# Eighteen stores of a hybrid encoder layer: issued by SyncE in place of ScalarE

## The chip, the cores and the metric

The kernel runs on one core of a Trainium2 chip. The metric is the device time of one execution in microseconds. A core has five engines with a queue of instructions each, worked off in order: TensorE (PE in the profile, its weight loads PEld), VectorE (DVE), ScalarE (ACT), GpSimd (POOL) and SyncE (SP). SyncE computes nothing; it issues transfers (DMA). ScalarE can issue transfers as well, from the same queue as its computing instructions. In the profile a queue's own work has a q behind the name: ACTq, SPq.

## The reference

One layer over 1040 tokens (16 meta tokens and 1024 of the sequence) of width 1024. A normalised input is projected once, and three mixers read the parts of the projection: a pooling mixer (256 columns), forgetting attention (6 heads of 64) and stick-breaking attention (6 heads of 64). Their outputs are concatenated, projected, added to the residual, and a SwiGLU network and a last norm follow.

```python
    for i in range(DEPTH):
        a = rmsnorm(h, norm1[i])
        proj = a @ w_in[i]
        u, qf, kf, vf, fl, qs, ks_, vs = jnp.split(proj, IN_SPLITS, axis=-1)
        y_pool = multiscale_pool_mixer(u, pool_w[i], pool_scale[i])
        ...
        y_fox = head_rmsnorm(y_fox, fox_out_gain[i], FOX_HEADS)
        ...
        y_sb = head_rmsnorm(y_sb, sb_out_gain[i], SB_HEADS)
        h = h + jnp.concatenate([y_pool, y_fox, y_sb], axis=-1) @ w_out[i]
        a = rmsnorm(h, norm2[i])
        h = h + (jax.nn.silu(a @ w_gate[i]) * (a @ w_up[i])) @ w_down[i]

    h = rmsnorm(h, final_norm)
    return h[:, N_META:N_META + s_len]
```

All inputs and the output are float32. The kernel keeps that accuracy by splitting each operand of a product into a rounded part and a rest (names with h and l: `wh`, `wl`, `ph`, `pl`, `dh`, `dl`) and adding three products.

## The kernel before, in words

The span has four parts: the input and its first projections, up to about 90 us; the mixers, to about 600 us; the SwiGLU network's first half, to about 1045 us; and its second half with the last norm. The change lies in the second part.

There the twelve heads are worked as six pairs, `p` = 0 to 5, in the order stick-breaking, three of forgetting attention, two of stick-breaking. For each pair `attention` computes scores (`sb_scores`, `fox_scores`), transposes them on TensorE, casts and subtracts them into two parts (lines 547 and 548, `ph` and `pl`), and multiplies by the values (line 533). When the two heads of a pair have half of the sequence (512 tokens) ready, `head_norm` normalises it: a square, two matmuls, logarithm and exponential on ScalarE, and a last multiply on VectorE (line 435) into the tile `yo`. `yo` has the tag `nt`, a ring of two tiles that the intermediate results of `head_out` (line 401) and of the norm use too. For the first five pairs `yo` is stored to a scratch tensor in HBM, `ysd` (line 572): ten stores of 256 KB. The sixth pair stays on the core.

Beside the attention runs a second stream, `filler`: the projections of the next pair (line 292), the two column blocks of the pooling mixer (`pool_pieces`) and the first parts of the output projection. The pooling mixer makes its output in four pieces for each of two blocks; ScalarE scales a piece out of PSUM (line 627) into a tile of tag `e`, a ring of three shared with the stick-breaking scores, and it is stored to `ysd` (line 628): eight stores of 124 to 132 KB. The output projection loads the halves of `ysd` again (`split_y`, line 697).

SyncE issues the loads of this part: the weights of the projections in pieces of 128 KB into a ring of four (`wr`, line 163; GpSimd splits each piece and so frees its buffer, line 167), the pool weights (line 614), the output weights and the scratch tensors' halves.

The order of instructions on each engine is not the order of the source. The framework's scheduler takes the whole program (`schedule_with_timeline_sim=True`), plays it through a model of the chip and gives each engine its next instruction by priority among those whose inputs and buffers are ready in the model. The function `interleave` sets how the two streams mix, and attention has a priority boost of 300. Semaphores are placed by the framework.

Of the kernel before, what the change touches and what calls it, by code (L numbers as in the profile page):

```python
# [30 lines left out]
def hymba_trunk(  # L31
# [19 lines left out]
    nc = tc.nc  # L51
# [12 lines left out]
    def T(p, shape, dt, tag, bufs=1):  # L64
        uid[0] += 1
        return p.tile(list(shape), dt, tag=tag, bufs=bufs, name=f"{tag}_{uid[0]}")
# [9 lines left out]
    def hi_pool(o, i):  # L76
        G.tensor_scalar(o, i, 1.0, 0.0, ALU.mult, ALU.add)
# [13 lines left out]
    def mm(tag, shape, bufs):  # L91
        return T(ps, shape, F32, tag, bufs)
# [82 lines left out]
    def wload(c):  # L175
        return wflat([wpart(c, hf) for hf in range(4)])
# [219 lines left out]
    def head_out(po, h, op):  # L396

        n = op.shape[1]
        a, b = 64 * h, 64 * (1 - h)
        t = T(at, [128, 512], F32, "nt", 2)  # L400
        S.copy(t[a:a + 64, :n], po[b:b + 64, :])
        V.tensor_tensor(op[a:a + 64, :], po[a:a + 64, :], t[a:a + 64, :n], ALU.add)
# [96 lines left out]
    def fox_bias(hd):  # L499
        cb = T(r1, [128, L], F32, "cb", 1)  # L500
        for t0, n in KPIECES:
            p = mm("s", [128, 512], SB_)
            PE.matmul(p[:, :n], sel[:, hd:hd + 1].to_broadcast([128, 128]), csum[:, t0:t0 + n], start=True, stop=True)
            S.copy(cb[:, t0:t0 + n], p[:, :n])
        return cb
# [22 lines left out]
    def weighted(pr, h, t, ptiles, po):  # L528
        nkb = 2 * t + 3

        def av(kb, xs, c, first):
            for ix, x in enumerate(xs):
                PE.matmul(po[:, c:256], pr.v[h][:, kb, :], x, start=first and ix == 0,  # L533
                          stop=(kb == nkb - 1 and ix == 1), skip_group_check=True)

        for g in range(0, nkb, 2):
            group = [(kb, ii) for kb in range(g, min(g + 2, nkb)) for ii in range(kb == nkb - 1, 2)]
            n = 128 * len(group)  # L540
            tp = mm("s", [128, 512], SB_)
            for i, (kb, ii) in enumerate(group):
                k0 = NM + 128 * (kb - 1) if kb else 0
                PE.transpose(tp[:, 128 * i:128 * i + 128], ptiles[ii][:, k0:k0 + 128], ident)  # L544
            ph = T(ap_, [128, 512], F32R, "ph", 3)
            pl = T(ap_, [128, 512], F32R, "pl", 3)
            S.copy(ph[:, :n], tp[:, :n])  # L547
            V.tensor_tensor(pl[:, :n], tp[:, :n], ph[:, :n], ALU.subtract)  # L548
            for kb in range(g, min(g + 2, nkb)):
                c = 128 if kb == nkb - 1 else 0  # L550
                a = 256 * (kb - g)
                av(kb, (ph[:, a:a + 256 - c], pl[:, a:a + 256 - c]), c, kb == 0)
            if kb < nkb - 1:
                yield 0.5

    def attention():

        pend = []
        cb = None
        ops = None  # L560

        def back(p, h, t, pts):
            fox, _, hd, c = PAIRS[p]
            po = mm("o", [128, 256], OB)
            yield from weighted(prs[p], h, t, pts, po)
            j, tt = t // 2, t % 2
            head_out(po, h, ops[j][:, 256 * tt:256 * tt + 256])
            if h == 1 and tt == 0:
                yo = T(at, [128, 512], F32, "nt", 2)
                head_norm(ops[j], c - 2, yo, p == 5 and j == 0, prs[p].lt[j] if fox else None)  # L570
                if p < 5:
                    nc.scalar.dma_start(ysd[c][:, 512 * j:512 * j + 512], yo)
                else:

                    yh, yl = [T(at, [128, 512], F32R, "q1", 6) if j else T(x0, [128, T0], F32R, "xb", 8)[:, :512]
                              for _ in range(2)]
                    (hi_pool if j else S.copy)(yh, yo)
                    V.tensor_tensor(yl, yo, yh, ALU.subtract)
                    last_y[j] = (yh, yl)
                    if j == 1:  # L580
                        yield None
            yield 0.5

        for p in range(6):
            fox, _, hd, c = PAIRS[p]
            if p:
                yield None
            if p == 5:
                seq = [(h, t) for t in (3, 2, 1, 0) for h in range(2)]
            else:  # L590
                seq = [(h, t) for h in range(2) for t in (3, 2, 1, 0)]
            for i, (h, t) in enumerate(seq):
                if fox and t == 3:
                    cb = fox_bias(hd + h)
                yield from (fox_scores if fox else sb_scores)(prs[p], h, t, cb)
                cur = (p, h, t, prs[p].pt)
                if i == 0:
                    while pend:
                        yield from back(*pend.pop(0))
                    ops = [T(at, [128, 512], F32, "op", 2) for _ in range(2)]  # L600
                pend.append(cur)
                while len(pend) > (DEEP[i] if p == 5 else 1):
                    yield from back(*pend.pop(0))
        while pend:
            yield from back(*pend.pop(0))


    def pool_pieces(ci):

        w = wload(ci)  # L610
        pw = T(ap_, [128, 512], F32, "e", 3)[:, :128]
        V.memset(pw, 0.0)
        for g in range(2):
            nc.sync.dma_start(pw[64 * g:64 * g + 64, 64 * g:64 * g + 64], pool_w[2 * ci + g])
        pwh = T(ap_, [128, 128], F32R, "pwh")
        S.copy(pwh, pw)
        pwl = T(ap_, [128, 128], F32R, "pwl")
        V.tensor_tensor(pwl, pw, pwh, ALU.subtract)
        late = []

        def mix(s0, n, dh, dl):
            p = mm("mm", [128, 512], MMB)
            PE.matmul(p[:, :n], pwh, dh[:, :n], start=True, stop=False)
            PE.matmul(p[:, :n], pwh, dl[:, :n], start=False, stop=False)
            PE.matmul(p[:, :n], pwl, dh[:, :n], start=False, stop=True)
            yo = T(ap_, [128, 512], F32, "e", 3)
            S.activation(yo[:, :n], p[:, :n], AF.Copy, scale=psc[:, ci:ci + 1])
            nc.scalar.dma_start(ysd[ci][:, s0:s0 + n], yo[:, :n])

        last = T(ap_, [128, NM], F32, "last")  # L630
        for t0, m in ((0, 264), (248, 280), (512, 272), (768, 272)):
            c0 = NM if t0 else 0
            o = []
            yield from proj_piece(w, t0 + c0, m - c0, o)
            u = T(at, [128, 512], F32, "pt", 3)
            if t0:
                G.tensor_copy(u[:, :NM], last)
            V.tensor_tensor(u[:, c0:m], o[0][:, :m - c0], rbc[:, t0 + c0:t0 + m], ALU.mult)
            if t0 + m < L:
                last = T(ap_, [128, NM], F32, "last")  # L640
                G.tensor_copy(last, u[:, m - NM:m])

            lv = []
            cur = u
            for lev in range(4 if ci else 2):
                sft = 1 << lev
                st = 2 * sft - 1
                nx = T(ap_, [128, 512], F32, "e", 3)
                lo = 64 if lev == (3 if ci else 1) else 0
                V.tensor_tensor(nx[lo:128, st:m], cur[lo:128, st:m], cur[lo:128, st - sft:m - sft], ALU.add)  # L650
                cur = nx
                lv.append(nx)
            n = m - NM
            dd = T(ap_, [128, 512], F32, "r", 3)
            for g in range(2):
                win = 2 << (2 * ci + g)
                r = slice(64 * g, 64 * g + 64)
                V.scalar_tensor_tensor(dd[r, :n], lv[-2 + g][r, NM:m], 1.0 / win, u[r, NM:m],
                                       ALU.mult, ALU.subtract)
            dh = T(ap_, [128, 512], F32R, "r", 3)  # L660
            hi_pool(dh[:, :n], dd[:, :n])
            dl = T(ap_, [128, 512], F32R, "r", 3)
            V.tensor_tensor(dl[:, :n], dd[:, :n], dh[:, :n], ALU.subtract)
            while late:
                mix(*late.pop())
            late.append((t0, n, dh, dl))
            yield 0.5
        while late:
            mix(*late.pop())
        yield 0.5  # L670
# [98 lines left out]
    ysd = {c: dpool.tile([128, SEQ], F32, name=f"ysd{c}") for c in range(8)}  # L769
# [446 lines left out]
```

## Time and profile before

| | |
|---|---|
| median of 3 runs | 1276.68 us (1276.63 to 1276.91) |
| profiled execution, its own time | 1277.83 us |
| its span, first to last instruction | 1275.8 us |
| mean granted clock of TensorE | 0.986 |
| TensorE busy | 1214.6 us |
| ScalarE busy | 624.4 us |
| issues of the 18 stores, on ScalarE's queue | 0.326 us each (median) |

Busy times count an engine's computing instructions; the issuing of a transfer is not among them. The chain of work that ended last is followed back from the last instruction, at each step to what released it; an engine with a small share in it can be slow at no cost. A timeline's row gives the start, the length, the engine, the line of the kernel, the operation, the tiles written and read, and in brackets the idle time before it with what ended it.

### The profile page before, as it was taken

To read this page: it belongs to the slowest core of one execution; us is meant where nothing else is said; L and a number is where in the kernel's file an instruction comes from. 1 tells how busy PE (TensorE), PEld (TensorE's weight loads), DVE (VectorE), ACT (ScalarE), POOL (GpSimd) and SP (SyncE) were. 2 spreads that over 40 slices of the span, in tenths; PEclk is the share of its full clock that TensorE was granted. 3 is DMA by queue.
4 is the path that set the end of the run, shared out by engine and by line. 5 is a ranking of instruction groups with operands and counts; after the bars stand their busy time and mean duration, and the time that the engine had idled before them with its cause. 6 is when DMAs were issued, how large, how long until landed. Compare 5 with 4: busy or idle time off the path is not lost.

```text
span 1275.8 us, 18424 instructions
## 1 busy us (share of the span) xinstructions
PE 1214.6 (95%) x6358; PEld 1024.7 (80%) x6358; DVE 915.9 (72%) x1568; ACT 624.4 (49%) x1272; POOL 489.5 (38%) x554
## 2 busy tenths in 40 slices
PE   6799899999899989999999999999999999999996
PEld 5588788889888877788787888888888888788885
DVE  8668975657947679998787677666767656866557
ACT  6366754545537677777744233233233324444443
POOL 6459245462355774550105444434444401000002
PEclk9899999999998999999999999999999999999999
DMA  5100011010101161201514554444555448576653
GB/s 181 41 9 30 19 48 34 30 38 18 47 30 34 34 219 64 78 26 50 205 42 158 190 168 169 141 130 152 190 173 165 140 140 323 174 229 196 190 169 140
DMA packets 73145, 147.12 MB, mean 115 GB/s; under 512 B 9052, under 2 KB 21340, under 8 KB 73052
## 3 DMA queue, kind: packets, MB, share of 16 engines
q1 hardware_dynamic: 69728, 142.01, 33.8%
q10 hardware_dynamic: 3324, 3.95, 0.9%
q8 instruction: 50, 0.82, 0.3%
q14 instruction: 43, 0.35, 0.1%
HBM read 103.98 MB, written 41.94 MB: 114 GB/s over the span
## 4 chain that ended last, share of the span: by engine, by line
PE 76%; DVE 14%; ACT 4%; issue 4%; DMA 1%; POOL 0%; POOLq 0%; SPq 0%; DVEq 0%; ACTq 0%
PE s L901 22%; PE mm L292 13%; PE s L1081 10%; PE mm L901 8%; PE mm L712 4%; PE o L533 4%; DVE r L490 3%; PE s L544 3%; PE mm L1081 3%; PE o L1081 3%; PE s L449 1%; DVE P L492 1%; DVE pl L548 1%; PE s L451 1%; DVE x L714 1%
## 5 line engine op out<-in xcount | busy, mean ns | idle before, releaser
L901 PE MATMUL s<-t,wh 128*128 128x512 f32 x544 | 168.7, 389 | 1.5 <-ACT wh L887 1.5
L901 PEld LDWEIGHTS s<-t,wh 128*128 128x128 f32 x544 | 101.9, 188 | 23.3 <-ACT wh L887 2.2
L901 PE MATMUL s<-s,wh 128*128 128x512 f32 x384 | 118.5, 390 | 0.9 <-ACT wh L887 0.9
L548 DVE TENSOR_TENSOR pl<-s,ph 128x512 fp32r<-128x512 f32 (+1 forms) x168 | 92.2, 568 | 36.2 <-ACT ph L547 32.1
L887 ACT CAST wh<-ss 128x512 fp32r<-128x512 f32 x80 | 49.5, 621 | 128.4 <-PE s L901 93.4
L547 ACT CAST ph<-s 128x512 fp32r<-128x512 f32 (+1 forms) x168 | 79.2, 494 | 63.3 <-PE o L533 34.6
L901 PE MATMUL s<-t,wl 128*128 128x512 f32 x272 | 105.6, 389 | 0.0
L292 PE MATMUL mm<-x,wh 128*128 128x512 f32 (+1 forms) x320 | 99.2, 383 | 0.4 <-DVE pt L357 0.4
L1069 ACT CAST wh<-sg 128x512 fp32r<-128x512 f32 x74 | 46.0, 623 | 108.9 <-PE s L1081 43.8
L901 PE MATMUL mm<-t,wh 128*128 128x512 f32 x320 | 98.6, 389 | 0.0
L1070 DVE TENSOR_TENSOR wl<-sg,wh 128x512 fp32r<-128x512 f32 x74 | 50.9, 689 | 61.4 <-ACT wh L1069 61.1
L887 ACT CAST wh<-raw 128x512 fp32r<-128x512 f32 x68 | 41.7, 620 | 106.2 <-PE s L901 67.7
L544 PE MATMUL s<-identr,P 128*128 128x128 f32 x528 | 82.6, 277 | 6.3 <-DVE pl L548 2.8
L901 PEld LDWEIGHTS s<-s,wh 128*128 128x128 f32 x384 | 72.0, 188 | 16.2 <-ACT wh L887 1.4
L995 DVE TENSOR_TENSOR cg<-s,tmp 128x512 f32<-128x512 f32 x60 | 41.3, 688 | 57.4 <-PE s L901 57.3
L533 PE MATMUL o<-pl,v 128*128 128x256 f32 (+1 forms) x288 | 81.8, 308 | 0.6 <-DVE pl L548 0.6
L1139 POOL TENSOR_SCALAR r<-ssq 128x1 f32<-128x1 f32 x7 | 2.9, 411 | 201.5 <-ACT fq L1138 201.5
L292 PE MATMUL mm<-xa,wh 128*128 128x264 f32 (+3 forms) x248 | 77.6, 315 | 1.0 <-ACT rbc L242 0.7
L533 PE MATMUL o<-ph,v 128*128 128x256 f32 (+1 forms) x288 | 77.0, 283 | 0.1
L292 PE MATMUL mm<-xb,wh 128*128 128x264 f32 (+3 forms) x248 | 76.9, 312 | 0.0
L292 PE MATMUL mm<-xa,wl 128*128 128x264 f32 (+3 forms) x248 | 76.7, 313 | 0.0
L544 PEld LDWEIGHTS s<-identr,P 128*128 128x128 f32 x528 | 62.6, 141 | 16.7 <-DVE pl L548 4.2
(292 smaller groups left out, 3577.0 us busy)
## 6 DMA issues: line engine op xcount, KB each, us to landing
sg<-lsd SPq DMA_DIRECT2D x70, 256.0 KB, 3.2
raw<-in_w_gate SPq DMA_DIRECT2D x22, 512.0 KB, 5.4
raw<-in_w_up SPq DMA_DIRECT2D x22, 512.0 KB, 3.7
wr<-in_w_in SPq DMA_DIRECT2D x80, 128.0 KB, 2.3
raw<-in_w_down SPq DMA_DIRECT2D x20, 512.0 KB, 3.5
lsd<-cg SPq DMA_DIRECT2D x40, 256.0 KB, 3.3
raw<-rsd SPq DMA_DIRECT2D x40, 256.0 KB, 3.6
raw<-in_w_down SPq DMA_DIRECT2D x34, 256.0 KB, 3.0
```

Of the source, the lines that this page charges most:

```text
L292: PE.matmul(p[:, :n], w[k][ww], xx(k, t0, n), start=i == 0, stop=i == 23)
L533: PE.matmul(po[:, c:256], pr.v[h][:, kb, :], x, start=first and ix == 0, stop=(kb == nkb - 1 and ix == 1), skip_group_check=True)
L544: PE.transpose(tp[:, 128 * i:128 * i + 128], ptiles[ii][:, k0:k0 + 128], ident)
L547: S.copy(ph[:, :n], tp[:, :n])
L548: V.tensor_tensor(pl[:, :n], tp[:, :n], ph[:, :n], ALU.subtract)
L712: PE.matmul(p, y_[:, ts_], w_[:, ds], start=i == 0, stop=i == 3 * len(ws) - 1)
L887: S.copy(wh, a)
L901: PE.matmul(p, ws[ww][:, k, :], xs_[xx][:, k, :], start=first and i == 0, stop=i == 11, skip_group_check=True)
L995: V.tensor_tensor(t, x, y, ALU.add)
L1069: S.copy(wh, a)
L1070: V.tensor_tensor(wl, a, wh, ALU.subtract)
L1081: PE.matmul(p, x[xx][:, 128 * b:128 * b + 128], y[yy], start=first and i == 0, stop=last and i == 2, skip_group_check=True)
```

## The change

Both stores are issued from SyncE's queue. The data, the sizes, the tiles and their destinations stay.

```diff
@@ -569,7 +569,7 @@
                 yo = T(at, [128, 512], F32, "nt", 2)
                 head_norm(ops[j], c - 2, yo, p == 5 and j == 0, prs[p].lt[j] if fox else None)
                 if p < 5:
-                    nc.scalar.dma_start(ysd[c][:, 512 * j:512 * j + 512], yo)
+                    nc.sync.dma_start(ysd[c][:, 512 * j:512 * j + 512], yo)
                 else:
...
@@ -625,7 +625,7 @@
             PE.matmul(p[:, :n], pwl, dh[:, :n], start=False, stop=True)
             yo = T(ap_, [128, 512], F32, "e", 3)
             S.activation(yo[:, :n], p[:, :n], AF.Copy, scale=psc[:, ci:ci + 1])
-            nc.scalar.dma_start(ysd[ci][:, s0:s0 + n], yo[:, :n])
+            nc.sync.dma_start(ysd[ci][:, s0:s0 + n], yo[:, :n])
```

## The prediction

> **What bounds the kernel now.** I read the page first, then the table by stretch, then the DMA issues, and last the timelines around single stores. The page:
>
> ```profile
> span 1275.8 us, 18424 instructions
> PE 1214.6 (95%) x6358; PEld 1024.7 (80%) x6358; DVE 915.9 (72%) x1568; ACT 624.4 (49%) x1272; POOL 489.5 (38%) x554
> PE 76%; DVE 14%; ACT 4%; issue 4%; DMA 1%; POOL 0%; POOLq 0%; SPq 0%; DVEq 0%; ACTq 0%
> ```
>
> TensorE is busy for 95% of the span and holds 76% of the chain of work that ended last. ScalarE holds 4%, its queue (ACTq, where the moved stores are issued) and SyncE's queue (SPq, where they go) each round to 0%. So the change touches two queues that end nothing today, and the question is what it does to TensorE's idle time. The next rows are the busy times by stretch, from 130 us to 570 us:
>
> ```profile
> 130.00:200.00 70.00, 62.22 (x433) 55.41 (x431) 55.43 (x135) 43.94 (x104) 27.62 (x47) 0.98 0.11 34
> 200.00:260.00 60.00, 59.46 (x397) 52.82 (x396) 37.01 (x108) 30.97 (x71) 27.71 (x45) 1.00 0.08 25
> 260.00:320.00 60.00, 59.76 (x424) 54.51 (x423) 40.90 (x114) 32.82 (x78) 28.04 (x44) 1.00 0.09 30
> 320.00:360.00 40.00, 36.53 (x262) 33.42 (x261) 32.84 (x90) 20.63 (x48) 15.41 (x27) 0.96 0.12 40
> 360.00:430.00 70.00, 67.22 (x414) 59.22 (x413) 44.56 (x92) 41.99 (x100) 42.90 (x62) 0.95 0.11 33
> 430.00:500.00 70.00, 65.83 (x392) 56.24 (x391) 54.24 (x94) 50.10 (x128) 47.20 (x54) 0.98 0.39 136
> 500.00:570.00 70.00, 66.81 (x354) 54.00 (x353) 66.79 (x107) 51.43 (x113) 36.16 (x33) 1.00 0.16 50
> ```
>
> The columns are the length, then busy time and count of PE, PEld, DVE, ACT and POOL, then the granted clock, the DMA share and GB/s. TensorE's busy times add to 417.83 of 440 us, so it idles 22.2 us in the part of the span in which all 18 stores lie. That is the whole stock that a better order of this part could win. It is uneven: 7.78 us are lost in 130:200 and 3.47 us in 320:360, against 0.54 and 0.24 us in the two stretches between them. The two poor stretches are those with the pool mixer's eight stores.
>
> **The change part by part.** Removed from ScalarE's queue: ten stores of a head norm (line 572) and eight of the pool mixer (line 628).
>
> ```profile
> L572 ACTq DMA_DIRECT2D ysd<-nt x10: 326/326/327, 168.1 to 531.3; - x10
> L628 ACTq DMA_DIRECT2D ysd<-e x8: 326/326/359, 153.8 to 350.4; - x8
> ```
>
> Each issue takes 0.326 us of ScalarE's queue, so 18 x 0.326 = 5.9 us are lifted from it. What of this sits on a path? The issue runs beside the engine's computation, so only idle time that ends with it counts. ScalarE's timeline around five stores:
>
> ```profile
> 153.72 0.29 ACT L481 ACTIVATE e<-s 128x144 f32<-128x144 f32 x1
> 153.84 0.36 ACTq L628 DMA_DIRECT2D ysd<-e  x1
> 154.25 0.32 ACT L486 ACTIVATE e<-e 128x144 f32<-128x144 f32 x1 [0.24 <-ACT e L481]
> 154.60 0.32 ACT L487 ACTIVATE e<-e 128x144 f32<-128x144 f32 x1
> ...
> 188.27 0.33 ACTq L572 DMA_DIRECT2D ysd<-nt  x1
> 190.52 0.59 ACT L547 CAST ph<-s 128x512 fp32r<-128x512 f32 x1 [3.06 <-PE o L533]
> ...
> 350.25 0.37 ACT L504 COPY cb<-s 128x264 f32<-128x264 f32 x1
> 350.39 0.33 ACTq L628 DMA_DIRECT2D ysd<-e  x1
> 350.75 0.38 ACT L504 COPY cb<-s 128x264 f32<-128x264 f32 x1
> ...
> 431.29 0.33 ACTq L572 DMA_DIRECT2D ysd<-nt  x1
> 431.77 0.54 ACT L494 ACTIVATE P<-P 128x400 f32<-128x400 f32 x1 [2.08 <-DVE P L492]
> ...
> 531.30 0.33 ACTq L572 DMA_DIRECT2D ysd<-nt  x1
> 531.67 0.59 ACT L547 CAST ph<-s 128x512 fp32r<-128x512 f32 x1 [1.67 <-PE s L544]
> ```
>
> At 153.84 the next Exp could have followed the Abs, which ends at 154.01, within the 0.03 us that separate lines 486 (ends 154.57) and 487 (starts 154.60); it starts at 154.25, so the store costs 0.21 us. At 350.39 the copy of line 504 ends at 350.62 and the next starts at 350.75: 0.13 less 0.03 is 0.10 us. At 531.30 the issue ends at 531.63 and the cast that waits for TensorE starts at 531.67, so at most 0.05 us is the store's. At 188.27 and 431.29 the engine stands at the store, which waits for VectorE's last multiply, but the work behind it then waits for TensorE until 190.5 and for VectorE until 431.77: nothing is won. The same holds for most of the rest. I take 0.36 us off ScalarE, from these three; its ends are 0, if none of it is on the path, and 5.9 us, if all 18 issues were. I take the low value because it is counted at the places, and ScalarE is 4% of the chain.
>
> Added to SyncE's queue: 18 issues of the same length. Two questions: do they delay the loads behind them, and do the loads ahead delay them? First the queue's waits from 130 to 445 us, then what GpSimd, which splits those loads, itself waits for on the loaded tile:
>
> ```profile
> SPq L163 <- POOL wl L167: 259.9, 48, 26.6
> ```
> ```profile
>   DMA wr<-in_w_in: 2.0, 1
> ```
>
> SyncE spends 259.9 us, in 48 waits, on waiting for GpSimd to give back a weight buffer, while GpSimd waited once, for 2.0 us, for a weight to arrive. The loads run far ahead; a slip of 0.3 us in one is covered by that lead, and costs at most the same 0.3 us if the lead is gone. The closest pair, with the widest gap behind it:
>
> ```profile
> 334.12 0.33 ACTq L628 DMA_DIRECT2D ysd<-e  x1
> 334.34 0.33 SPq L163 DMA_DIRECT2D wr<-in_w_in  x1
> ...
> 335.95 0.33 SPq L163 DMA_DIRECT2D wr<-in_w_in  x1
> ...
> 341.00 0.33 ACTq L572 DMA_DIRECT2D ysd<-nt  x1
> 343.18 0.37 ACT L401 COPY nt<-o 64x256 f32<-64x256 f32 x1
> 349.49 0.37 ACT L401 COPY nt<-o 64x256 f32<-64x256 f32 x1
> ...
> 360.89 0.33 SPq L163 DMA_DIRECT2D wr<-in_w_in  x1
> ```
>
> A store at 334.12 would hold SyncE until 334.45 and shift the load at 334.34 by 0.11 us: hidden, zero. The store at 341.00 falls in a gap between issues at 335.95 and 360.89; if the queue's order keeps it ahead of the load at 360.89, SyncE can issue it on the spot, and I take that (the order of stores and loads in the kernel's own queues is by the same planner). The price if not is a rival below. The transfer itself:
>
> ```profile
> ysd<-nt ACTq DMA_DIRECT2D x10, 256.0 KB, 2.0
> gsd<-sg SPq DMA_DIRECT2D x4, 256.0 KB, 2.0
> ```
>
> A store of the same 256 KB from SyncE's queue to a scratch tensor lands in the same 2.0 us, so the two-deep ring of the output tile (nt) comes free no later. In 130:430 the DMA share is 0.08 to 0.12, so no queue of transfers is in the way. Zero.
>
> Moved indirectly: the planner that lays down each engine's order decides afresh from the first moved store on. No row shows another order, so I bound it: for the gain by the 22.2 us of idle, for the loss by the worst stretch repeated (7.8 us in 70 us). Which way it falls the trace doesn't say, and I take zero, the value that two stretches with almost no idle time suggest for a part whose binding engine keeps all its work.
>
> Sum: -0.36 + 0 + 0 = -0.4 us. The profiled execution took 1277.83 us, 2.0 us around its span of 1275.8; the median of the runs is 1276.68, 1.15 us below that execution, and the saving is taken off the median: 1276.3 us.
>
> The row says 0.36 of 5.9 us. The Trainium skill, "DMA: Bandwidth & Descriptors", section "Issuing engines are not separate DMA queues", says that the queues share the 16 DMA engines and that spreading issues over several engines saves only the sequencer's time to start them. By that rule the most there is to win is 5.9 us, if ScalarE's time counted in full; and the equal 2.0 us landing from both queues agrees with it.
>
> **The rivals.** (0.2% is 2.55 us here, about what separates a change from none.)
>
> *The issue time counts in full.* ScalarE's casts feed TensorE's weighted sums, and if each 0.326 us delayed a chain of cast, subtract and matmul, 5.9 us go: 1270.8. Against it: in the five places above 0.36 us of idle time end with the store. Chance 0.05.
>
> *The new order is better.* If half of the idle time of the two pool stretches (7.78 + 3.47 = 11.25 us) closes, the time is 1276.3 - 5.6 = 1270.7. For it: the stretches between lose 0.8 us in 120, so such an order exists. Against: nothing in the change aims at it. Chance 0.26.
>
> *The new order is worse.* One good stretch takes on half of what 130:200 loses beyond it, 3.6 us: 1279.9; with a whole one, 1283.5. Chance 0.20.
>
> *A store stuck behind a load.* In order on SyncE, a store that stands behind the load at 360.89 instead of ahead of it is issued at 361.2 and lands at 363.2. Its tile is one of two; ScalarE's copy at 343.18 takes the other, that of 349.49 needs this one and would stand until 363.2, 13.7 us, with ScalarE and the attention behind it: 1290. It decides as soon as one store of the ten slips past a load that waits over 8 us (349.49 less 341.00). Against it: where the stores are issued today agrees with the loads' gaps. Chance 0.08.
>
> **How the numbers follow.** No measurable change has 0.41 and gives the time, 1276.3, with its own range 1274.1 to 1279.2. Faster is 0.05 + 0.26 = 0.31, slower 0.20 + 0.08 = 0.28. The range goes down to 1270.5, which takes in both prices of the faster cases, and up to 1283, near the whole bad stretch; beyond it lie the stuck store and the tails of a new order, together under 0.2.
>
> **What would show it.** After: 18 issues of line 572 and 628 on SPq, landing in about 2.0 us; SyncE's waits still for GpSimd; ACT's share of the chain still near 4%; TensorE's idle time in 130:570 near 22 us. The copy of line 401 waiting for a store's landing would show the stuck store; an idle time that moved by 4 us or more with the same operations, the new order. What makes the forecast wrong is above all that order, which no row here can fix.

## The result and the profile after

The changed kernel takes 1282.05 us (median of 5 runs, 1280.13 to 1284.61); the kernel before, run beside it, 1276.68 us (median of 5 runs, 1274.87 to 1277.78). The ratio is 1.0047, 95% interval [1.0034, 1.0060]: slower by about 6 us. The profiled execution took 1280.13 us, the fastest of its five.

The page of the kernel after, the rows that answer to those shown of before:

```profile
span 1278.1 us, 18414 instructions
PE 1216.2 (95%) x6358; PEld 1025.0 (80%) x6358; DVE 912.8 (71%) x1568; ACT 624.6 (49%) x1272; POOL 490.3 (38%) x554
PE 71%; DVE 14%; issue 5%; ACT 5%; DMA 4%; POOL 0%; POOLq 0%; SPq 0%; DVEq 0%; ACTq 0%
```

Each engine works off the same number of computing instructions as before (the counts behind the x), in busy times that differ by less than 0.4%, and SPq and ACTq still have nothing in the chain. The DMA issues of the kernel after (tile written and read, count, KB each, median us from issue to landing) and the longest waits of SyncE's queue from 130 to 445 us:

```profile
ysd<-nt SPq DMA_DIRECT2D x10, 256.0 KB, 2.0
ysd<-e SPq DMA_DIRECT2D x4, 128.0 KB, 1.9
ysd<-e SPq DMA_DIRECT2D x2, 132.0 KB, 2.1
ysd<-e SPq DMA_DIRECT2D x2, 124.0 KB, 2.0
```
```profile
SPq L163 <- POOL wl L167: 172.8, 44, 15.6
SPq L572 <- DVE nt L435: 27.8, 5, 18.4
...
SPq L628 <- ACT e L627: 12.3, 3, 7.2
```

All 18 stores are on SyncE and land as fast as before. SyncE now stands for some of them until their data are there (27.8 us in five waits for the multiply of line 435), and less for GpSimd (172.8 us against 259.9). Does that cost the mixers anything? The table by stretch, same columns as before:

```profile
130.00:200.00 70.00, 62.81 (x431) 55.88 (x432) 53.31 (x132) 43.46 (x104) 26.88 (x46) 0.98 0.11 34
200.00:260.00 60.00, 59.47 (x399) 52.78 (x398) 36.45 (x110) 30.47 (x71) 29.87 (x48) 1.00 0.08 25
...
320.00:360.00 40.00, 36.95 (x257) 33.40 (x256) 31.44 (x88) 20.50 (x47) 15.49 (x29) 0.96 0.12 40
...
sum 440.00, PE 420.27 PEld 366.67 DVE 329.20 ACT 272.09 POOL 226.46; mean PE 60.04 PEld 52.38 DVE 47.03 ACT 38.87 POOL 32.35
```

TensorE idles 440 - 420.27 = 19.7 us there, against 22.2 us before. The part of the span that the change touches did not get slower. The loss comes behind it, from 600 us on, where no store was moved. Comparing the order of instructions on each engine shows why it can: the scheduler laid down a new order. Of 3438 matmuls of the mixers' part some 620 stand elsewhere; further on, 47 matmuls in the tail (the last output projection, mixed with the first products of the SwiGLU network, the "direct" ones of the function `direct`) and ten instructions in the late part (680 to 700 us: six matmuls, two of VectorE, one of ScalarE, one issue of SyncE).

*The tail.* After the mixers TensorE mixes the last products of the output projection (line 712) with the direct SwiGLU products (line 901). The changed kernel issues 37 of the latter ahead of the last of the former, the kernel before 31. Both reach the end of line 712 at the same time (630.35 us before, 630.32 after), although the changed kernel began the direct products 1.9 us earlier (613.54 against 615.44). From that end a chain goes on, here in four timelines of the kernel before:

```profile
630.39 0.69 DVE L714 TENSOR_TENSOR x<-mm,x 128x512 f32<-128x512 f32 x1 [1.63 <-PE mm L712]
...
665.65 0.68 DVE L1049 TENSOR_TENSOR sg<-raw 128x512 f32<-128x512 f32 x1
...
666.37 0.32 SPq L1052 DMA_DIRECT2D rsd<-sg  x1
666.78 0.38 SPq L894 DMA_DIRECT2D raw<-in_w_gate  x1
...
670.53 1.29 POOL L1000 TENSOR_TENSOR ss<-raw 128x512 f32<-128x512 f32 x1 [37.36 <-DMA raw<-in_w_gate]
...
673.20 1.85 ACT L887 CAST wh<-ss 128x512 fp32r<-128x512 f32 x3 [0.19 <-POOL ss L983]
```

VectorE adds the residual, normalises and splits until 665.65, then makes what SyncE stores (line 1052); the load of the gate weights stands right behind that store in SyncE's queue, GpSimd waits for its landing, ScalarE casts, and TensorE waits for the cast. TensorE's rows, first before, then after:

```profile
671.95 0.39 PE L901 MATMUL mm<-t,wl 128*128 128x512 f32 x1
673.88 1.25 PE L901 MATMUL s<-t,wh 128*128 128x512 f32 x4 [1.54 <-ACT wh L887]
```
```profile
670.47 0.39 PE L901 MATMUL mm<-t,wl 128*128 128x512 f32 x1
673.95 1.25 PE L901 MATMUL s<-t,wh 128*128 128x512 f32 x4 [3.09 <-ACT wh L887]
...
676.10 0.63 PE L901 MATMUL s<-t,wl 128*128 128x512 f32 x1
```

The changed kernel comes to this place 1.5 us earlier and waits 1.5 us longer: what it was ahead by is lost.

*The clock.* The last row above has a single matmul of 0.63 us where 0.39 is usual. The granted clock is in the table by stretch (the column behind the five engines), of before and of after:

```profile
675.00:678.40 3.40, 3.40 (x16) 2.82 (x16) 3.40 (x4) 2.16 (x5) 2.70 (x2) 1.00 0.02 5
```
```profile
675.00:678.40 3.40, 3.40 (x10) 2.62 (x10) 3.40 (x5) 2.18 (x5) 2.63 (x2) 0.59 0.02 5
```

Behind the longer gap the clock falls, and ten matmuls are done where sixteen were.

*The late places.* VectorE's add of line 990, for whose tile TensorE waits, starts at 681.78 before and at 684.73 after (it now stands behind the differences of lines 1050 and 1051); the difference of line 1049, which waits for a load, now stands ahead of work that is ready (5.68 us of idle time before it, against 4.08). Two new gaps on TensorE in the kernel after:

```profile
684.73 0.68 DVE L990 TENSOR_TENSOR tmp<-s,tmp 128x512 f32<-128x512 f32 x1
...
695.20 0.69 DVE L1049 TENSOR_TENSOR sg<-raw 128x512 f32<-128x512 f32 x1 [5.68 <-DMA raw<-in_w_down]
```
```profile
685.46 0.74 PE L901 MATMUL s<-t,wh 128*128 128x512 f32 x2 [0.33 <-DVE tmp L990]
697.15 0.73 PE L901 MATMUL s<-s,wh 128*128 128x512 f32 x2 [0.70 <-DVE cg L995]
```

Measured by the starts of the same matmuls in both traces, the changed kernel is some 4 us ahead at 600 us, 1.89 us ahead at 615 us (in between, from 607.34 us, its clock is at half for 3.41 us, which the trace of before does not have), 0.08 behind at 674, 3.34 behind at 715 and, one us given back near 1090, 2.28 behind at the end. The two profiled executions differ by 2.3 us, the medians by 5.4; executions of one kernel lie mostly within 3 us of their median, a few further off, so single traces show where, and the ratios how much.

### The profile page after: what moved, and what is told of

It reads as the page before. It is cut to its first block, busy times and chain, and to the rows that moved or that the text cites. A ratio compares the mean times of both kernels' runs of the same rounds, so it can differ in the third digit from the quotient of the medians.

```text
span 1278.1 us, 18414 instructions
## 1 busy us (share of the span) xinstructions
PE 1216.2 (95%) x6358; PEld 1025.0 (80%) x6358; DVE 912.8 (71%) x1568; ACT 624.6 (49%) x1272; POOL 490.3 (38%) x554
## 4 chain that ended last, share of the span: by engine, by line
PE 71%; DVE 14%; issue 5%; ACT 5%; DMA 4%; POOL 0%; POOLq 0%; SPq 0%; DVEq 0%; ACTq 0%
PE s L901 20%; PE mm L292 13%; PE s L1081 8%; PE mm L901 8%; PE mm L712 4%; PE o L533 4%; DVE r L490 3%; PE s L544 3%; PE mm L1081 3%; PE o L1081 3%; PE s L449 2%; PE s L451 1%; DVE P L492 1%; DVE x L714 1%; DVE pl L548 1%
```

## The experiments

Theory R: the planner's new order costs the time, and which engine issues the stores costs nothing. Its rival Q: the queue costs it. Within R, theory T says that the tail costs it, and theory L that the ten late places do. Kernels called "held" carry a list of the recorded order of each engine and tie every instruction to its predecessor; that adds no wait between engines, only a fixed order:

```python
    for ...:                      # the instructions in the recorded order
        i = code[at_]
        prior = before_.get(str(i.engine))
        if prior is not None:
            tc.add_manual_dep(i, prior.name, ...NoSync...)
        before_[str(i.engine)] = i
```

In held kernels a line number is 2 higher than in the kernel before; in the kernels `sp_cut18`, `act_cut18` and `act_cut12` below it is 1 higher from line 767 on and 6 higher from line 956 on.

**The stores on SyncE, every engine in the order of before.** `sp_order_before`: the changed kernel with the list of the kernel before.

> The 18 stores on SyncE, but every engine is held to the order of instructions of the kernel before; the stores stand in SyncE's queue between the same loads between which ScalarE issued them. Theory R (the loss is the planner's new order, the change of queue itself moves nothing): 1276.3 us, 1274.5 to 1278.0. Rival Q (SyncE's queue costs: stores hold up loads, or tiles come free later): the loss is here already, 1280 to 1284.

Measured: 1276.01 us against 1275.73, ratio 0.9997 [0.9984, 1.0011]. Its chain of waits:

```profile
PE 74%; DVE 13%; issue 5%; ACT 5%; DMA 3%; POOL 0%; POOLq 0%; SPq 0%; DVEq 0%; ACTq 0%
```

The queue costs nothing that can be measured. The chain's shares differ from those of before here too (PE 74% against 76%, DMA 3% against 1%; the changed kernel has 71% and 4%), at no cost: by themselves such shifts are no sign of the loss.

**The stores on ScalarE, all in the order of after.** `act_order_after`: the kernel before with the list of the changed kernel.

> The 18 stores on ScalarE as before, but every engine is held to the order that the planner laid down for the changed kernel. Theory R: as slow as the changed kernel, 1280 to 1284 us, with TensorE's gap of about 3 us near 671 us and VectorE standing 5 to 6 us at line 1049 near 690 us. Rival Q: 1275 to 1278.

Measured: 1281.54 us, ratio 1.0043 [1.0027, 1.0059]. The loss is there without the change. Together the two leave R, and Q falls.

**Only the mixers in the new order.** `sp_mixers_after`: stores on SyncE, the list of after for the mixers, that of before for the tail and the late part.

> Stores on SyncE, the mixers' part in the changed kernel's order, all that is written behind it (last output projection, SwiGLU, last norm) in the order of before. Theory T (the new order of the mixers gains about 1.5 us and the loss sits in the tail and behind it): 1274 to 1276.5 us. Rival M (the new order of the mixers is itself worse, and the later stalls follow from it): 1280 to 1283.

Measured: 1276.92 us, ratio 1.0006 [0.9996, 1.0016]. The matmuls that moved in the mixers cost nothing measurable. They win nothing either: the 1.5 us that theory T gave them from the trace are not there, and the median lies 0.4 us above its range.

**Only the late places put back.** `sp_late_before`: the changed kernel, held, with the ten late places of before.

> The changed kernel with only the order from the SwiGLU's Strassen products on as before: six matmuls, two VectorE instructions, one of ScalarE and one issue on SyncE (the store of line 1052 behind the load of w_up) stand elsewhere. Theory L (these ten places cost what the trace loses between 680 and 700 us, about 1.7 us): 1279.5 to 1281. If all of the loss hangs on them: 1276 to 1277.5. If none: 1282.

Measured: 1279.80 us, ratio 1.0037 [1.0022, 1.0052]. Most of the loss stays, so the late places are not its whole cause; the interval overlaps that of the changed kernel, so what putting them back wins is not resolved.

**Only the tail in the new order.** `act_tail_after`: the kernel before, held, with 47 matmuls, six VectorE, three ScalarE and one SyncE place of the tail as after.

> Stores on ScalarE and the order of before everywhere but in the last output projection and the direct SwiGLU products behind it (the tail, 600 to 670 us), which stand in the changed kernel's order. Theory T (the tail's new order starts SwiGLU products ahead of the output projection that VectorE's long chain waits for; TensorE then stands longer near 671 us): slower by 1.5 to 3.5 us, 1277.2 to 1279.2, and the last output product ends 1.5 us or more later after the start of the first SwiGLU product than the 14.9 us of before. Rival S (the tail alone costs nothing, the loss needs the changed mixers ahead of it): 1275 to 1276.5.

Measured: 1279.95 us against 1275.62, ratio 1.0034 [1.0021, 1.0047]: more than either range. The profiled execution (1283.46 us) is the slowest of the ten, so its trace shows what can happen and not the median cost. TensorE's row shows the same gap as after, and the stretch behind it the clock at half:

```profile
678.40 2.08 PE L903 MATMUL s<-t,wh 128*128 128x512 f32 x4 [3.11 <-ACT wh L889]
```
```profile
678.40:682.00 3.60, 3.60 (x9) 2.82 (x10) 3.60 (x4) 2.29 (x5) 2.31 (x3) 0.50 0.02 5
```

**Only the late places in the new order.** `act_late_after`: the kernel before, held, with those ten places as after.

> Stores on ScalarE and the order of before everywhere but in the ten places behind the tail (six matmuls, two VectorE instructions, one of ScalarE, and the store of line 1052 ahead of a load of w_up on SyncE). Theory L: these cost 1.3 to 2 us, so 1277 to 1277.8, seen as VectorE standing over 5 us before line 1049 and TensorE waiting near 695 us. Rival S (the late places cost only behind a TensorE that is already late): 1275 to 1276.3.

Measured: 1279.21 us, ratio 1.0030 [1.0018, 1.0042], a miss: 1.4 us above the range of theory L. In the trace (1282.27 us, the slowest of the twelve), with the tail of before, TensorE comes to the add of line 990 (here 992) in time, and waits for it longer than in the changed kernel; then the clock falls here too:

```profile
686.67 0.76 PE L903 MATMUL s<-t,wh 128*128 128x512 f32 x2 [1.94 <-DVE tmp L992]
```
```profile
688.00:692.00 4.00, 4.00 (x13) 3.12 (x12) 2.80 (x3) 0.62 (x1) 3.29 (x3) 0.67 0.64 210
```

By the matmuls, 3.87 us are lost between 675 and 720 us in this trace. This may also be why the parts don't add (0.34% and 0.30%, but 0.43 to 0.47% together), which no run tests by itself: in the changed kernel TensorE is already late from the tail, and waits only 0.33 us for line 990. The load of the up weights that SyncE issues 6 us later in this order, on which my expectation dwelt, ended no wait of TensorE in this trace.

**Only the head norms' stores on SyncE.** `only_norms`: the edit of line 572 alone, the planner free.

```diff
-                    nc.scalar.dma_start(ysd[c][:, 512 * j:512 * j + 512], yo)
+                    nc.sync.dma_start(ysd[c][:, 512 * j:512 * j + 512], yo)
```

> Only the ten stores of the head norms are moved to SyncE; the planner decides freely, and lays down the changed kernel's order in the tail and in most of the late places, though not the store ahead of the load on SyncE. Theories R and T: slower by 3 to 5.5 us, 1279 to 1281. A theory by which each store moved costs the same: 10/18 of the loss, 1278.7.

Measured: 1282.54 us, ratio 1.0057 [1.0041, 1.0073], 1.5 us above the range; a theory of an equal price for each store (1278.7 us) falls. TensorE waits 2.96 us at the same place. The ten stores of line 572 suffice to make the planner choose the slow tail.

**Only the pool mixer's stores on SyncE.** `only_pool`: the edit of line 628 alone, in the same manner (`nc.scalar` to `nc.sync`).

> Only the eight stores of the pool mixer are moved to SyncE; the planner changes the mixers' order (some 400 matmuls stand elsewhere) but leaves the tail and all behind it as before. Theories R and T: no change, 1274.5 to 1277. A theory by which each store moved costs the same: 8/18 of the loss, 1278.1.

Measured: 1274.84 us, ratio 1.0005 [0.9990, 1.0021]: 413 matmuls of the mixers moved, tail and late part as before, no change in time.

**Only TensorE's places of the tail.** `act_tail_pe_after`: the kernel before, held, with the 47 matmuls of the tail as after and the places of the other engines as before.

> Every engine in the order of the kernel before, stores on ScalarE, but TensorE's 47 moved places of the tail as in the changed kernel; the six VectorE, three ScalarE and one SyncE places of the tail stay as before. If TensorE's order alone makes the tail slow: what the whole tail gave, 1278.5 to 1280.5 us, 1.0022 to 1.0038. If the places on VectorE, ScalarE and SyncE make it: 1275 to 1277 us.

Measured: 1280.95 us against 1275.89, ratio 1.0034 [1.0022, 1.0045], the same as with the whole tail. TensorE's order alone makes it.

**Fewer direct products ahead, in the changed kernel.** `sp_cut18`: the planner is free, but ties the direct products from the 19th on behind the last product of line 712. The mixers stay in the order of after, and the late places come out as before.

```diff
-                    PE.matmul(p, y_[:, ts_], w_[:, ds], start=i == 0, stop=i == 3 * len(ws) - 1)
+                    last_out[0] = PE.matmul(p, y_[:, ts_], w_[:, ds], start=i == 0, stop=i == 3 * len(ws) - 1)
...
     for c in PAIR0:
         direct(c, 1)
+    for i in [x for x in code[first:] if str(x.engine) == str(last_out[0].ins.engine)][18:]:
+        tc.add_manual_dep(i, last_out[0].ins.name, ...NoSync...)
```

> The changed kernel with one rule more in its planner: only 18 of the direct SwiGLU products, in place of 37, may be issued by TensorE ahead of the last product of the output projection (line 712 of the kernel before). The mixers keep the order of the changed kernel; the ten late places come out as in the kernel before. If the late end of the output projection is what makes the tail slow (theory T): 19 products of 0.23 us less in its way are 4.4 us, the 3.1 us for which TensorE waits near 671 us close, the granted clock does not fall at 675 us, and the last late loads go out as before: 1274 to 1276 us, 0.997 to 1.001 against the kernel before. If the place of the output projection is not the cause and any new order of the tail costs what the changed one does: 1279 to 1281 us.

Measured: 1275.99 us, ratio 1.0001 [0.9989, 1.0013]. The loss is won back with the stores on SyncE and the mixers in the new order. The clock at 675 us doesn't fall. But the gap does not close:

```profile
671.61 1.26 PE L902 MATMUL s<-t,wh 128*128 128x512 f32 x4 [1.25 <-ACT wh L888]
```

**The same rule in the kernel before**, with 18 and with 12 products ahead: `act_cut18`, `act_cut12`.

> The kernel before, stores on ScalarE, with the same rule: 18 direct products, in place of 31, ahead of the last product of the output projection. The mixers keep their order of before; two late matmuls, one late ScalarE and one late VectorE instruction move too. Theory T: the output projection ends 13 times 0.23 = 3.0 us earlier, and the 1.54 us for which TensorE waits near 671 us close: 1273.5 to 1275.5 us, 0.9980 to 1.0000. If the gap at 671 us is set by something else (the landing of the gate weights, the number of products left for the wait): 1275.5 to 1280 us.

> The same with 12 direct products ahead of the output projection's end. Theory T: no more to win than with 18, since the gap of 1.54 us is all that stands there, 1273.5 to 1275.5 us; if TensorE then waits within the output projection itself for its operands (which the direct products filled): slower than with 18 by up to 2 us, 1275 to 1278 us.

Measured: 1276.25 us, ratio 0.9998 [0.9987, 1.0008], and 1274.83 us, ratio 0.9993 [0.9982, 1.0004]. No gain that can be told from none: theory T's claim that the 1.54 us would close was wrong. The gap becomes 1.25 us in both, and ScalarE's timeline (of the kernel with 18) says why:

```profile
671.76 0.58 ACT L1011 COPY tmp<-mm 128x512 f32<-128x512 f32 x1 [7.62 <-PE mm L902]
672.24 1.66 ACT L888 CAST wh<-ss 128x512 fp32r<-128x512 f32 x3
```

The weights are there earlier (GpSimd starts to split them at 668.02 in place of 670.53), but the cast stands in ScalarE's queue behind a copy that waits for TensorE's last product. Copy, cast and hand-over are the 1.25 us that no earlier load removes. The runs side by side, times in us from each kernel's own trace:

| kernel | direct products start | line 712 ends | between | GpSimd has the gate weights | gap on TensorE |
|---|---|---|---|---|---|
| before | 615.44 | 630.35 | 14.91 | 670.53 | 1.54 |
| after | 613.54 | 630.32 | 16.78 | 670.64 | 3.09 |
| only the tail as after | 617.85 | 634.67 | 16.82 | 675.10 | 3.11 |
| only TensorE's tail as after | 615.64 | 633.06 | 17.42 | 673.28 | 2.90 |
| after, 18 products ahead | 612.75 | 625.44 | 12.69 | 667.86 | 1.25 |
| before, 18 products ahead | 614.49 | 626.77 | 12.28 | 668.02 | 1.25 |
| before, 12 products ahead | 615.86 | 626.75 | 10.89 | 668.18 | 1.25 |

From the end of line 712 to the weights it is 40 to 42 us in every row. None of these versions is shown to beat the kernel before.

## Why the prediction was wrong

The steps on the change itself held.

- *ScalarE relieved of 5.9 us, 0.36 us of it on the path; 18 issues on SyncE hidden; equal landing.* With the order fixed these sum to a ratio of 0.9997 [0.9984, 1.0011], which covers the -0.4 us; the landing is 2.0 us for the head norms' stores and 1.9 to 2.1 us for the pool mixer's. The issue time as such was worth nothing measurable, which answers the rule quoted from the Trainium skill ("DMA: Bandwidth & Descriptors", "Issuing engines are not separate DMA queues"): the saving is at most the sequencer's time, and here not even that showed.
- *The store stuck behind a load* did not happen. The changed kernel's SyncE queue around the place where the rival was priced:

```profile
338.48 0.33 SPq L628 DMA_DIRECT2D ysd<-e  x1
339.18 0.33 SPq L572 DMA_DIRECT2D ysd<-nt  x1
349.56 0.32 SPq L628 DMA_DIRECT2D ysd<-e  x1
359.60 2.33 SPq L163 DMA_DIRECT2D wr<-in_w_in  x2
```

The store of line 572 goes out ahead of the load, as the prediction took it.

- *"Moved indirectly: the planner ... decides afresh ... I take zero"* is the step that failed. It was 0.47% [0.34, 0.60], and the case that came about is the rival "the new order is worse", whose prices (1279.9 for half of a bad stretch, 1283.5 for a whole one) enclose the measured time. It got a chance of 0.20. That its prices fit is luck: they were taken from idle time of the mixers, where the new order cost nothing.
- The bound of that step was also taken from the wrong place. I looked for the new order where the stores are, from 130 to 570 us; there it won 2.5 us of TensorE's idle time in the trace and nothing measurable as an experiment (1.0006 [0.9996, 1.0016]). It lost behind, from 600 to 700 us, in places of no connection to a store. "A part whose binding engine keeps all its work" was no reason for zero: the part that lost kept its work too, but TensorE's order there decides when VectorE's chain of 35 us begins.
- Two things that "What would show it" named misled: TensorE's idle time in 130:570 near 22 us was there (19.7), and the 4 us by which it should have moved as the sign of a new order were not, although the new order was the cause. ACT's share of the chain stayed near 4% (5%), as forecast.
- The size: longer gaps explain only part of it. It is best read from the trace of only TensorE's tail as after, whose execution (1280.66 us) lies near its median (1280.95). Against the same matmuls of before it loses 1.8 us between 600 and 660 us, where the direct products that were drawn ahead wait themselves, in one case for a weight (the row below; the trace of before has no such wait). It loses 1.4 us in the gap (2.90 against 1.54 us) and 1.4 us behind it, where the clock is at half (0.50 from 676.59 to 680.00 us). Near 1090 us 1.1 us come back. So this trace shows 3.5 us; the ratio says 4.3 us, with an interval from 2.8 to 5.7.

```profile
618.76 0.50 PE L903 MATMUL s<-s,wl 128*128 128x512 f32 x1 [0.97 <-DVE wl L891]
```

Does the clock always fall behind the longer gap? All fourteen traces have a gap at this place. In the eight with the tail of before or with fewer products ahead it is 1.25 to 1.60 us long, and the clock does not fall directly behind it. In the six with the changed kernel's tail it is 2.90 to 3.11 us long, and behind five of them the clock falls. The sixth is the changed order with the late places put back:

```profile
673.42 1.25 PE L903 MATMUL s<-t,wh 128*128 128x512 f32 x4 [2.92 <-ACT wh L889]
```
```profile
675.00:678.40 3.40, 3.40 (x17) 2.75 (x16) 3.40 (x4) 1.79 (x4) 3.15 (x2) 1.00 0.00 0
```

That execution took 1276.47 us, the fastest of that kernel's seven (median 1279.80). This fits a price paid in most executions.

The traces also show what spared it. In each trace the granted clock changes only at times that are whole multiples of 3.41 us apart: in the changed kernel's it falls at 607.34 and at 675.61 us, 20 such steps later. As far as the traces show, what counts is how TensorE's idle time lies on these steps. The rows (TensorE's busy time stands right behind the length) are one step of the changed kernel (the one ahead of its fall), one of the kernel with only the late places as after (it holds the whole gap of 1.94 us), two of the kernel that was spared (its gap of 2.92 us is cut in two), and one of the kernel before:

```profile
672.19:675.61 3.42, 1.66 (x6) 1.08 (x7) 1.68 (x3) 2.24 (x5) 2.29 (x2) 1.00 0.02 5
```
```profile
683.84:687.25 3.41, 1.47 (x7) 0.88 (x7) 3.41 (x6) 1.14 (x2) 0.42 (x1) 1.00 0.65 156
```
```profile
668.88:672.29 3.41, 1.62 (x8) 1.00 (x6) 0.00 (x0) 0.59 (x1) 2.11 (x2) 1.00 0.72 287
672.29:675.70 3.41, 2.28 (x9) 1.55 (x10) 2.30 (x4) 2.81 (x5) 2.12 (x3) 1.00 0.02 5
```
```profile
670.40:673.81 3.41, 1.94 (x9) 1.28 (x7) 0.00 (x0) 1.19 (x3) 3.20 (x3) 1.00 0.44 171
```

Between 600 and 700 us of the fourteen traces the clock fell behind nine steps at full clock, in which TensorE was busy for 0.54 to 1.66 us; it stayed full behind the one step of 1.62 us shown here and behind all with 1.74 us or more. So in these traces the border lies near half a step, and a gap of 3 us is spared only when a boundary cuts it near its middle.

What stays open: whether that border holds elsewhere (in the mixers of the changed kernel the clock fell at 160.19 us behind a step with 2.24 us busy). Why the planner, given ten stores in another queue, takes six more products ahead of the end of the output projection, over 80 us behind the last of these stores, was not followed either.

## What to carry to other kernels

Where a scheduler orders the whole program by playing it through a model, an edit of one line is two changes: the edit, and a new order of everything behind it. Hold each engine to the recorded order and measure the edit alone, then give the old kernel the new order; these two runs say which it is. Bound the second from all places where a long chain hangs on one engine's order (here the end of the output projection), not only from the stretch that the edit touches, and put a loss of half a per cent among the likely cases.

## What the runs showed of the hardware

TensorE's granted clock can fall to half behind a short idle time, for one step of 3.41 us, or for two: with only the tail as after it stood at 0.50 from 677.47 to 684.29 us. Matmuls of 128x512 then take 0.63 us in place of 0.39, and nine to ten are done in 3.4 to 3.6 us in place of 16 to 18. From 600 us on it was seen behind gaps of 1.94 us and of 2.90 to 3.11 us and, in some traces, of 1.68 us with more idle time in the same step; it was not seen behind 1.25 to 1.60 us and one of 2.92 us. As far as these traces show, what decided was how long TensorE was busy in a step of the grid on which the clock changes: the border lay at 1.6 to 1.7 us of 3.41. A gap of 2 to 3 us on the engine that binds can therefore cost up to about twice its length (3.87 us around the gap of 1.94 us).

The Trainium skill ("TensorE: Matmul & The Clock Gate", "What's actually happening") puts the half clock behind an idle window of about 3.4 us. These traces differ: it fell behind steps in which TensorE had still worked for up to 1.66 us. The same section of the Trainium skill describes the window as free-running, which agrees with the grid of 3.41 us and with a gap that sometimes costs and sometimes doesn't.
